# Evictions of the in-projection without the scheduling mark, and three rearrangements around the down-projection

## The chip, the cores and the metric

The kernel runs on one core of one Trainium2 chip. The metric is the device time of one execution in microseconds (us). A core has TensorE (PE in the profile, with PEld for its weight loads), VectorE (DVE), ScalarE (ACT), GpSimd (POOL) and SyncE (SP), which here issues most of the transfers. Each engine works through its own queue in order and waits on semaphores for the others. A time is told by three runs of the kernel before: 2315.92, 2316.55 and 2322.16 us, median 2316.55.

## The reference

One step of a hybrid layer, all in fp32, for 2048 prompt tokens and 8 short sample sequences of 16 tokens: 17 tiles of 128 tokens with 1024 features each. In short:

```
z = x @ w_in                    # 1024 -> mLSTM q, k, v, o-gate, gates; attention q, k, v
h = mlstm_chunkwise(...)        # 4 heads x 128, then a norm per head times the o-gate
a = swa(...)                    # 8 query heads on 2 key heads, window of two chunks, rotary, sinks
x = LN(alpha * x + concat(h, a) @ w_out)
u = causal_conv3(x @ w_up)      # 1024 -> 2 x 2816, value and gate
y = LN(alpha * x + (silu(gate) * value) @ w_down)
```

It returns y for the prompt and the samples, and the new states and key/value rows.

## The kernel before

Each fp32 operand is split in two parts that TensorE takes at full rate: `split` casts to the high part on ACT (L217) and subtracts for the low part on DVE (L218). A product is then three matmuls: high by high, high by low, low by high. The large matrix products are also cut in 2 x 2 blocks and computed with seven block products instead of eight (Winograd's form of Strassen's method). Sums of blocks are made on DVE before, and sums of results while they are evicted from PSUM. Several results share a PSUM bank by being copied from one bank to another and added onto.

The order of TensorE's instructions is written out by hand. On the other engines a scheduler orders them by what is ready and by priority. `tc.high_priority()` marks instructions so that they go ahead of others; `tc.issue_after(x)` keeps instructions behind instruction x.

Stages, in the time of the profile:

- In-projection, about 0 to 634 us (L704, `i_product`; sample tiles L714; direct tiles L730). Four token blocks b, in each five column groups g, in each seven products s of 24 matmuls with 256 columns. The products of a group run in the order 6, 7, 2, 5, (1 of the next group), 3, 4. They share three banks: A for s = 1 and 2, B for 6, 5, 3, and C for 7, 4. `i_after` evicts after each product. After s = 6 ACT copies B (the lines L763 to L771, the forms that scale, copy or apply tanh). After s = 2 it evicts A. After s = 5 it copies B and DVE adds C to it (L775, L777). After s = 3 ACT evicts B and then copies A onto B (L799), which the next group's product 6 adds to. After s = 4 DVE adds C once more. A product that writes a bank waits for those that read it. Chains of the mLSTM (L1083 to L1244: decay dt and wi, pnum, the head statistics L1149, hn, pht) and of the attention (L1303 to L1359: scores sc, softmax L1307 to L1324, ppt, pth) run between these products, with their ACT and DVE work in the same queues. POOL takes one square root of variance per head group there (L1161).
- `d_sums` runs beside the in-projection: block sums of the down-projection's weights. For each of eleven pairs k, step 0 loads two weight tiles `txy` into buffers that otherwise hold tokens (L844, L845), step 1 makes four sums of 512 columns on DVE (L850 to L853), and step 2 stores both to DRAM (`zt`, L855, L856). Eight pairs are made in blocks 2 and 3 of the in-projection, three in the output projection.
- Output projection (`o_block`), about 634 to 870 us, with the last chains (ppt L1346).
- Up-projection, about 870 to 1884 us (L1877, `f_ups`): three token blocks, 22 column pairs j, seven products. `f_evict` makes value and gate u from the banks (ACT L1898 to L1912, DVE L1906, L1908, L1914), and DVE, ACT and POOL compute the convolution and the gate (L1928 to L1960). In the last products the program already prepares the down-projection: `d_weights` loads a weight unit (L2023) and splits it into `uw`, `d_tokens` splits a token unit into `fu`.
- Down-projection, about 1847 to 2317 us (L2087, `f_downs`): for each block seven products of six units. DVE adds finished products into the rows `yacc` (L2116, L2118), and the last norm follows in pieces. The last tile is finished by `norm_last`: statistics in two halves (L1559), aggregate (L1560), a power on POOL (L1562), and then two passes over 512 columns each (L1545, L1547), stored one by one.

Of the kernel before, what the change touches and what calls it, by code (L numbers as in the profile page):

```python
# [14 lines left out]
P = 128  # L15
# [189 lines left out]
class Prog:  # L205
# [381 lines left out]
    def i_dense(self):  # L587
# [34 lines left out]
        for item in self.items:  # L622
            if after:

                after[0] -= 1
                if after[0] == 3:
                    self.logs_of(after[1] - 1)
                if after[0] < 0:
                    self.i_done = after[1]
                    after = None  # L630
            self.chains.hold = item[0] == "t" and item[1] > 0
            if item[0] == "t":
                _, b, ti, e = item
                if ("g", e, 3) not in self.wu:
                    self.advance()
                if b not in self.gates:
                    self.gates[b] = self.tp.tile([P, 5, 8], F32, name="gates", tag="gates", bufs=2)
                ps = self.bank([P, 512], "pg") if ti == 4 else self.ib[ti % 2 * 2]
                yield from self.i_direct(b, ti, e, ps)
                self.i_keys(b, ti, ps)  # L640
                if ti == 1:
                    if b + 1 < nb:
                        self.x_steps(b + 1, 1, 2)
                    else:
                        self.release(4)
# [12 lines left out]
            del self.wu[item]  # L658
            self.release(2)
            if self.trans and s != 4:  # L660
                self.i_transposes()
            with self.tc.high_priority():
                behind = self.i_after(b, g, s)
            if (b, g, s) == (0, 0, 7):
                self.t_setup()
            if (g, s) == (1, 6):
                self.rope_load(IBLOCKS[b][0], 2)
            if g == last and b + 1 < nb:
                if s == 7:
# [12 lines left out]
            if b >= nb // 2 and g < last:  # L682

                steps = (6, 2, 5) if g == last - 1 else (6, 5, 3)
                if s in steps:
                    self.d_sums(sums, steps.index(s))
                    sums += s == steps[2]
        self.sums = sums
        self.logs_of(nb - 1)
        self.chains.hold = False  # L690
# [846 lines left out]
        self.mix_out(t, 4, mix)  # L1537


    def norm_last(self, y, g, bb, dst, st):  # L1540

        nc, V = self.nc, self.nc.vector
        mv, s = self.stats(y, st)
        for c in (slice(0, 512), slice(512, 1024)):
            V.scalar_tensor_tensor(y[:, c], y[:, c], mv[:, 0:1], g[:, c], op0=ALU.subtract, op1=ALU.mult)  # L1545
        for c in (slice(0, 512), slice(512, 1024)):
            V.scalar_tensor_tensor(y[:, c], y[:, c], s[:, 0:1], bb[:, c], op0=ALU.mult, op1=ALU.add)  # L1547
            nc.sync.dma_start(dst[:, c], y[:, c])

    def stats(self, y, st=None):  # L1550
        nc = self.nc
        V = nc.vector
# [5 lines left out]
        for i in range(half, 2):  # L1558
            V.bn_stats(st[:, i], y[:, i * 512:(i + 1) * 512])  # L1559
        V.bn_aggr(mv, st)  # L1560
# [255 lines left out]
    def f_ups(self, n):  # L1816
# [11 lines left out]
        for i, (b, j, s) in enumerate(self.seq):  # L1828
# [25 lines left out]
                self.d_begin()  # L1854

            left = len(self.seq) - i
            if left in (8, 7, 5, 3, 1):
                self.d_weights()
            if left in (9, 8, 7, 6):
                self.d_tokens()  # L1860
        nc.sync.dma_start(self.a["conv_p"], self.prev.rearrange("p v j r -> p (v j) r"))
        nc.sync.dma_start(self.a["conv_s"], self.convs.rearrange("p v j b r -> p (v j) b r"))

# [15 lines left out]
    def f_evict(self, b, j, s):  # L1879
# [22 lines left out]
        elif s == 5:  # L1902
            self.ug = u = half(1)
            u4 = f2.tile([P, 384], F32, name="ub", tag="ub", bufs=1)[:, :h]
            S.copy(u4, B)
            V.tensor_add(u[:, 2 + h:2 + WP], C[:, :m], u4[:, :m])  # L1906
            if has_s:
                V.tensor_add(sam(u)[:, :, 2:], dec(C), dec(u4))  # L1908
        elif s == 3:
            S.copy(self.uv[:, 2 + h:2 + WP], B[:, :m])  # L1910
            if has_s:
# [144 lines left out]
    def f_downs(self):  # L2056
# [17 lines left out]
        nb, nu = len(FBLOCKS), len(DUNITS)  # L2074
        ys, ops = {}, {}
        last_tile = FBLOCKS[-1][0]
        st = self.wp.tile([P, 2, 6], F32, name="st", tag="st", bufs=1)

        def product(s, p, units):
            ps = banks[role[s][2 if p == np_ else p]]  # L2080
            c = slice(p * P, p * P + P)
            for u in units:
                wh, wl, fh, fl = ops[u]
                n = len(DUNITS[u])
                for k in range(n):
                    for i, (l, r) in enumerate(((fh, wh), (fh, wl), (fl, wh))):
                        mm(ps, l[:, k, c], r[:, k], start=s in (1, 4, 7) and u == 0 and k == 0 and i == 0,  # L2087
                           stop=u == nu - 1 and k == n - 1 and i == 2, skip_group_check=True)

        def after(s, p):  # L2090
# [5 lines left out]
            elif s == 2:  # L2096
                add(ta, 0, ps, True)
                if ta == last_tile:
                    V.bn_stats(st[:, 0], ys[ta][:, :512])
# [19 lines left out]

        def finish(t, b, step):  # L2120
            if b == nb - 1 and step == 3:
                self.norm_last(ys[t], *ln2, a["y"][t], st if t == last_tile else None)
                return
            y, (g, bb) = ys[t], ln2
            mv, sc = self.stats(y)
# [8 lines left out]
        for g, (b, s, u) in enumerate(self.dseq):  # L2134
# [16 lines left out]
                    product(s, p, [u])  # L2151
            elif u == 0:
                cols = cols[::-1]
                for p in cols:
                    product(s, p, [u])
            elif u == nu - 1:

                cols = cols[::-1]
                for p in cols:
                    product(s, p, range(1, nu))  # L2160
                    after(s, p)
                    for _ in pending.pop():
                        pass

            for f in pending[:2]:
                if next(f, self) is self:
# [23 lines left out]
```

## Time and profile before

| | |
|---|---|
| median of three runs | 2316.55 us (2315.92 to 2322.16) |
| the profiled execution, its own time | 2321.38 us |
| span of its trace | 2319.6 us |
| mean granted TensorE clock | 0.995 |
| busy: TensorE, weight loads | 2287.3 us, 2097.9 us |
| busy: DVE, ACT, POOL | 1818.9, 1273.3, 267.8 us |
| moved by DMA | 632.39 MB, 273 GB/s |

A row of the timeline has the start and the duration in us, the engine, the line, the operation, out <- in, and the count of instructions that the row joins; a bracket gives the idle time before the row and what released it. Consecutive instructions on one engine overlap a little, so that in a row of them each takes some 0.1 us less than the duration shown. A row of waits has the waiting instruction, what released it, the sum in us, how often, and the longest. A row of windows has the window, its length, the busy time of each engine with its count, the granted clock, the DMA share and GB/s.

### The profile page before, as it was taken

To read this page: it belongs to the slowest core of one execution; us is meant where nothing else is said; L and a number is where in the kernel's file an instruction comes from. 1 tells how busy PE (TensorE), PEld (TensorE's weight loads), DVE (VectorE), ACT (ScalarE), POOL (GpSimd) and SP (SyncE) were. 2 spreads that over 40 slices of the span, in tenths; PEclk is the share of its full clock that TensorE was granted. 3 is DMA by queue.
4 is the path that set the end of the run, shared out by engine and by line. 5 is a ranking of instruction groups with operands and counts; after the bars stand their busy time and mean duration, and the time that the engine had idled before them with its cause. 6 is when DMAs were issued, how large, how long until landed. Compare 5 with 4: busy or idle time off the path is not lost. (4 is left out here: it accounts for less than half of the span.)

```text
span 2319.6 us, 39851 instructions
## 1 busy us (share of the span) xinstructions
PE 2287.3 (99%) x14293; PEld 2097.9 (90%) x14293; DVE 1818.9 (78%) x3189; ACT 1273.3 (55%) x2409; POOL 267.8 (12%) x477
## 2 busy tenths in 40 slices
PE   8999999999999999999999999999999999999998
PEld 8999989899977778999999999999999978888876
DVE  7777687787688888998788777678766786895987
ACT  5453466776766665555556555556555544444442
POOL 0001000100011112121102000003111200100200
PEclk9999999999999999999999999999999999999999
DMA  7888999989986767788777888888998776756743
GB/s 270 289 304 294 302 311 329 313 300 327 334 279 225 234 210 271 286 327 310 279 293 270 307 306 307 314 269 283 313 297 265 227 286 205 258 176 218 258 153 109
DMA packets 300166, 632.39 MB, mean 273 GB/s; under 512 B 47868, under 2 KB 141120, under 8 KB 299968
## 3 DMA queue, kind: packets, MB, share of 16 engines
q1 hardware_dynamic: 295296, 616.14, 77.5%
q0 software_dynamic: 3520, 10.56, 1.4%
q10 hardware_dynamic: 1152, 3.15, 0.4%
q8 instruction: 113, 1.85, 0.3%
q14 instruction: 85, 0.70, 0.1%
HBM read 458.11 MB, written 171.64 MB: 271 GB/s over the span
## 5 line engine op out<-in xcount | busy, mean ns | idle before, releaser
L1877 PE MATMUL dps<-hh,uw 128*128 128x384 f32 (+1 forms) x1848 | 478.1, 328 | 2.6 <-DVE u L1908 2.0
L1877 PE MATMUL fup<-hh,uw 128*128 128x384 f32 (+1 forms) x1848 | 478.1, 328 | 0.3 <-ACT ua L1898 0.2
L1877 PEld LDWEIGHTS dps<-hh,uw 128*128 128x128 f32 x1848 | 329.9, 188 | 3.1 <-DVE u L1908 2.3
L1877 PEld LDWEIGHTS fup<-hh,uw 128*128 128x128 f32 x1848 | 330.0, 188 | 0.8 <-ACT ua L1898 0.5
L1934 DVE SCALAR_TENSOR_TENSOR cc<-u,cw,cc 128x768 f32<-128x768 f32 (+1 forms) x264 | 258.2, 979 | 60.9 <-ACT cc L1932 51.8
L1877 PE MATMUL fup<-hl,uw 128*128 128x384 f32 (+1 forms) x924 | 302.5, 327 | 1.8 <-DVE hl L218 1.8
L1877 PE MATMUL dps<-hl,uw 128*128 128x384 f32 (+1 forms) x924 | 302.3, 327 | 0.0
L704 PE MATMUL dps<-w,oh 128*128 128x256 f32 x1344 | 254.9, 284 | 1.2 <-DMA w<-zws 0.7
L217 ACT CAST uw<-wraw 128x1024 fp32r<-128x1024 f32 x126 | 123.1, 979 | 222.8 <-PE dps L2087 120.1
L218 DVE TENSOR_TENSOR w<-wraw,w 128x1024 fp32r<-128x1024 f32 (+2 forms) x167 | 189.3, 1141 | 50.4 <-ACT w L217 45.7
L704 PEld LDWEIGHTS dps<-w,oh 128*128 128x128 f32 x1344 | 210.6, 188 | 12.7 <-issue 8.1
L217 ACT CAST w<-wraw 128x1024 fp32r<-128x1024 f32 (+2 forms) x167 | 163.2, 984 | 102.9 <-PE dps L704 37.3
L218 DVE TENSOR_TENSOR uw<-wraw,uw 128x1024 fp32r<-128x1024 f32 x126 | 142.5, 1132 | 64.3 <-ACT uw L217 64.3
L704 PE MATMUL dps<-w,ol 128*128 128x256 f32 x672 | 187.9, 280 | 0.0
L704 PE MATMUL dps<-oh,w 128*128 128x256 f32 x896 | 172.5, 287 | 6.2 <-ACT mr L1152 3.4
L1877 PEld LDWEIGHTS fup<-hl,uw 128*128 128x128 f32 x924 | 173.5, 188 | 2.5 <-DVE hl L218 2.4
L2087 PE MATMUL fup<-uw,fu 128*128 128x512 f32 x726 | 174.0, 396 | 0.6 <-DVE uw L218 0.6
L1877 PEld LDWEIGHTS dps<-hl,uw 128*128 128x128 f32 x924 | 173.5, 188 | 0.0
L2087 PEld LDWEIGHTS fup<-uw,fu 128*128 128x128 f32 x726 | 136.3, 188 | 34.0 <-DVE uw L218 1.1
L2087 PE MATMUL dps<-uw,fu 128*128 128x512 f32 x660 | 165.3, 396 | 1.1 <-DVE uw L218 1.1
L1932 ACT ACTIVATE cc<-u,cw 128x768 f32<-128x768 f32 (+1 forms) x132 | 132.2, 1001 | 52.6 <-DVE u L1914 26.7
L704 PEld LDWEIGHTS dps<-oh,w 128*128 128x128 f32 x896 | 143.5, 192 | 12.7 <-issue 4.1
(322 smaller groups left out, 4588.6 us busy)
## 6 DMA issues: line engine op xcount, KB each, us to landing
uw<-zw SPq DMA_DIRECT2D x176, 512.0 KB, 5.2
zw<-uw SPq DMA_DIRECT2D x88, 512.0 KB, 3.6
w<-zws SPq DMA_DIRECT2D x72, 512.0 KB, 6.4
wv<-wup SPq DMA_DIRECT2D x66, 512.0 KB, 4.8
wraw<-wi SPq DMA_DIRECT2D x65, 512.0 KB, 5.3
wraw<-zt SPq DMA_DIRECT2D x60, 512.0 KB, 4.3
wraw<-wdn SPq DMA_DIRECT2D x45, 512.0 KB, 4.2
wraw<-wo SPq DMA_DIRECT2D x40, 512.0 KB, 4.7
```

The source lines that it names most:

```text
L217: nc.scalar.copy(hi, src)
L218: nc.vector.tensor_sub(lo, src, hi.bitcast(F32))
L704: mm(o, l, r, start=s in (1, 7) and c == k == i == 0, stop=k == 3 and i == 2, skip_group_check=True)
L1877: mm(ps, l[:, k], r[:, k], start=s in (1, 7) and k == 0 and i == 0, stop=k == 3 and i == 2, skip_group_check=True)
L1932: S.activation(c[:, v], u[:, 2:2 + n], AF.Identity, bias=w[3], scale=w[2])
L1934: V.scalar_tensor_tensor(c[:, v], u[:, i:i + n], w[i], c[:, v], op0=ALU.mult, op1=ALU.add)
L2087: mm(ps, l[:, k, c], r[:, k], start=s in (1, 4, 7) and u == 0 and k == 0 and i == 0, stop=u == nu - 1 and k == n - 1 and i == 2, skip_grou ...
```

## The change

Four edits:

1. `i_after` is called without `high_priority`, so that the scheduler treats evictions as it treats other work.
2. The steps of `d_sums` stand behind other products: load after s = 7, sums after s = 3, store after s = 4. The first of the eight pairs moves from block 2 to the fourth group of block 1; the next three stay in block 2, the last four in block 3.
3. In the last products of the up-projection the calls of `d_tokens` and `d_weights` are placed otherwise, and two calls of `d_weights` and one of `d_tokens` are kept behind the last sums onto u (`u4_add`).
4. The last product of the last tile (s = 3, p = 0) is done in two halves of 256 columns. The second half's partial sum is copied by ACT to another bank at the product's first unit. The 33 matmuls of 512 columns become 66 of 256. The first half is added and its statistics are taken beside the second half's matmuls; after the last matmul stand an add and statistics of 256 columns and the aggregate over four groups.

```diff
-            with self.tc.high_priority():
-                behind = self.i_after(b, g, s)
+            behind = self.i_after(b, g, s)
...
-            if b >= nb // 2 and g < last:
-                steps = (6, 2, 5) if g == last - 1 else (6, 5, 3)
-                if s in steps:
-                    self.d_sums(sums, steps.index(s))
-                    sums += s == steps[2]
+            if s in (7, 3, 4) and (b == nb - 1 and g < last or b == nb - 2 and g < last - 1 or b == 1 and g == last - 2):
+                self.d_sums(sums, (7, 3, 4).index(s))
+                sums += s == 4
...
-            if left in (8, 7, 5, 3, 1):
+            if left in (9, 8, 7):
+                self.d_tokens()
+            if left in (8, 7):
                 self.d_weights()
-            if left in (9, 8, 7, 6):
-                self.d_tokens()
+            if left in (4, 2):
+                with self.tc.issue_after(self.u4_add):
+                    self.d_weights()
+                    if left == 4:
+                        self.d_tokens()
+            if left == 1:
+                self.d_weights()
...
-            V.tensor_add(u[:, 2 + h:2 + WP], C[:, :m], u4[:, :m])
+            z = V.tensor_add(u[:, 2 + h:2 + WP], C[:, :m], u4[:, :m])
             if has_s:
-                V.tensor_add(sam(u)[:, :, 2:], dec(C), dec(u4))
+                z = V.tensor_add(sam(u)[:, :, 2:], dec(C), dec(u4))
+            self.u4_add = z.ins
...
-        def product(s, p, units):
-            ps = banks[role[s][2 if p == np_ else p]]
+        def product(s, p, units, cs=slice(0, 512), ps=None):
+            ps = banks[role[s][2 if p == np_ else p]][:, cs] if ps is None else ps
...
-                        mm(ps, l[:, k, c], r[:, k], start=s in (1, 4, 7) and u == 0 and k == 0 and i == 0,
+                        mm(ps, l[:, k, c], r[:, k, cs], start=s in (1, 4, 7) and u == 0 and k == 0 and i == 0,
...
+                halves = [(slice(i * 256, i * 256 + 256), banks[(role[s][0], 0)[i]][:, :256]) for i in range(2)]
+                S.copy(halves[1][1], banks[role[s][0]][:, 256:])
                 for p in cols:
-                    product(s, p, [u])
+                    for cs, ps in halves if p == 0 else [(slice(0, 512), None)]:
+                        product(s, p, [u], cs, ps)
...
-                for p in cols:
+                for p in cols[:-1]:
                     product(s, p, range(1, nu))
                     after(s, p)
                     for _ in pending.pop():
                         pass
+                for i, (cs, ps) in enumerate(halves):
+                    product(s, 0, range(1, nu), cs, ps)
+                    y = ys[last_tile][:, 512 + i * 256:768 + i * 256]
+                    V.scalar_tensor_tensor(y, y, ALPHA, ps, op0=ALU.mult, op1=ALU.add)
+                    V.bn_stats(st[:, 2 + i], y)
+                self.norm_last(ys[last_tile], *ln2, a["y"][last_tile], st)
```

The statistics tile `st` of the last tile accordingly has four groups instead of two, and its first half is taken in two pieces of 256 columns.

More of the change, by code (lines that the diff above doesn't have):

```diff
@@ L1537, in swa_sample, with norm_last @@
         self.mix_out(t, 4, mix)
-    def norm_last(self, y, g, bb, dst, st):
+    def norm_last(self, y, g, bb, dst, st=None):
         nc, V = self.nc, self.nc.vector
@@ L1557, in stats @@
         s = self.wp.tile([P, 2], F32, name="lsc", tag="lsc", bufs=2)
-        for i in range(half, 2):
-            V.bn_stats(st[:, i], y[:, i * 512:(i + 1) * 512])
+        if st.shape[1] == 2:
+            for i in range(half, 2):
+                V.bn_stats(st[:, i], y[:, i * 512:(i + 1) * 512])
         V.bn_aggr(mv, st)
@@ L2076, in f_downs @@
         last_tile = FBLOCKS[-1][0]
-        st = self.wp.tile([P, 2, 6], F32, name="st", tag="st", bufs=1)
-        def product(s, p, units):
-            ps = banks[role[s][2 if p == np_ else p]]
+        st = self.wp.tile([P, 4, 6], F32, name="st", tag="st", bufs=1)
+        def product(s, p, units, cs=slice(0, 512), ps=None):
+            ps = banks[role[s][2 if p == np_ else p]][:, cs] if ps is None else ps
             c = slice(p * P, p * P + P)
@@ L2098, in after @@
                 if ta == last_tile:
-                    V.bn_stats(st[:, 0], ys[ta][:, :512])
+                    for i in range(2):
+                        V.bn_stats(st[:, i], ys[ta][:, i * 256:i * 256 + 256])
             elif s in (4, 6):
```

2 lines of the change are left out of this document (1 added, 1 removed).

## The prediction

> **What bounds the kernel now.** I read the page's busy times first, then the chain of waits of TensorE (PE), then windows with the granted clock, then the timelines at each place where an engine's order changes.
>
> The page, and TensorE's waits by the line that waited and what released it (total us, times, longest):
>
> ```profile
> PE 2287.3 (99%) x14293; PEld 2097.9 (90%) x14293; DVE 1818.9 (78%) x3189; ACT 1273.3 (55%) x2409; POOL 267.8 (12%) x477
> ...
> L704 PEld LDWEIGHTS dps<-w,oh 128*128 128x128 f32 x1344 | 210.6, 188 | 12.7 <-issue 8.1
> ...
> PE dps L704 <- ACT mr L1152: 3.4, 1, 3.4
> PE dps L1877 <- DVE u L1908: 2.0, 1, 2.0
> ...
> PE ppt L1346 <- ACT sc L1324: 1.5, 1, 1.5
> ...
> PE ppt L1521 <- POOL scs L1515: 0.8, 1, 0.8
> ...
> PE fup L2087 <- DVE uw L218: 0.6, 1, 0.6
> ...
> PE pht L1178 <- ACT hn L1168: 0.5, 1, 0.5
> ```
>
> PE is busy 2287.3 of 2319.6 us, so 32 us of idle time is all that reordering can win, besides time lost to a low clock. The windows (length, PE, PEld, DVE, ACT, POOL, granted clock, DMA share, GB/s) show that loss:
>
> ```profile
> 328.60:332.40 3.80, 0.36 (x4) 0.15 (x3) 3.65 (x15) 1.70 (x5) 0.00 (x0) 0.80 0.73 243
> 332.40:337.60 5.20, 5.20 (x24) 5.20 (x25) 5.20 (x15) 2.49 (x6) 0.00 (x0) 0.50 1.08 306
> ...
> 692.50:696.00 3.50, 3.50 (x13) 2.93 (x12) 3.01 (x9) 2.67 (x8) 1.59 (x2) 0.53 1.00 369
> ...
> 1840.00:1850.00 10.00, 8.00 (x46) 7.12 (x45) 9.91 (x15) 5.18 (x8) 6.11 (x8) 1.00 0.52 172
> ```
>
> After the 3.44 us wait the clock is 0.50 for 5.2 us, half of which is lost; behind the 1.5 us wait, which ends just before 692.5, it is 0.53 for 3.5 us (1.7 lost). The window of 1840 holds the 2.0 us wait (PE 8.00 of 10.00) at clock 1.00, so a wait of that length need not cost more than itself. The Trainium skill ("TensorE: Matmul & The Clock Gate", HAM oscillation) allows idle gaps up to about 3.4 us. The first wait agrees; the one of 1.5 us does not. By that rule alone the stalls of 1 to 2 us that I find below never halve the clock; by the rows they may (second rival).
>
> **The change, part by part.** *Evictions without the mark, and sums moved.* Both act through the queues of ACT and DVE, so they are walked together. Decisive rows, up to the late head (ACT, DVE, PE, POOL timelines):
>
> ```profile
> 316.63 0.59 ACT L771 ACTIVATE zev<-dps 128x512 f32<-128x512 f32 x1
> ...
> 320.48 0.39 ACT L1318 ACTIVATE sc<-sc,amx 128x128 f32<-128x128 f32 x1
> ...
> 326.87 1.27 ACT L1324 ACTIVATE sc<-sc,asm 128x128 f32<-128x128 f32 x4
> ...
> 320.91 0.67 DVE L1131 TENSOR_TENSOR dt<-pscore,dt 128x512 f32<-128x512 f32 x1
> 321.51 1.20 DVE L218 TENSOR_TENSOR w<-wraw,w 128x1024 fp32r<-128x1024 f32 x1
> ...
> 327.27 0.69 DVE L850 TENSOR_TENSOR txy<-txy 128x512 f32<-128x512 f32 x1 [3.32 <-DMA txy<-wdn]
> ...
> 320.55 0.39 PE L704 MATMUL dps<-oh,w 128*128 128x256 f32 x2
> ...
> 320.89 0.39 PE L704 MATMUL dps<-oh,w 128*128 128x256 f32 x2
> ...
> 321.69 1.13 PE L1213 MATMUL pnum<-v,dt 128*128 128x129 f32 x8 [0.18 <-issue]
> ...
> 328.66 0.28 PE L704 MATMUL dps<-oh,w 128*128 128x256 f32 x1
> 332.38 0.58 PE L704 MATMUL dps<-oh,w 128*128 128x256 f32 x1 [3.44 <-ACT mr L1152]
> ...
> 341.22 0.75 PE L1178 MATMUL pht<-ident,hn 128*128 128x128 f32 x4
> ...
> 337.78 1.47 POOL L1161 TENSOR_TENSOR ms<-mq,mhalf 128x4 f32<-128x4 f32 x1 [13.64 <-DVE mq L1160]
> ```
>
> The 3.44 us stall begins on DVE: it waits 3.32 us at L850 for a weight tile (issued too late for its place), so L1149's statistics and ACT's mr (L1152) are late, and the eviction L771 stands behind them. The change puts that pair's sums elsewhere, so the DVE wait leaves. But L771 of 316.63 now stands behind five attention activations (L1316, four L1318) of which the last ends at 320.9; with its own 0.59 it ends near 321.5, while the product that overwrites its bank began at 320.66 (the second matmul of the row of 320.55): new stall 0.8. On DVE the split (1.20) now precedes dt (L1131): it ends about 322.7 and the pnum of 321.69 begins near 322.8 (these 1.1 us include the 0.8). The next two products end at 330.05 instead of 328.94. The second L771 (it ended just before the 332.38) now follows eight L1324 softmax divisions, one cast and both mr on ACT. From 327.0, where ACT's earlier work ends in the new order, that is 8 x 0.3 (1.27 for four) + 1.0 for the cast (as 1.20 on DVE, a little less on ACT) + 0.2 + 0.6: about 331.2, and I allow 331.0 to 331.5. So a stall of 1.0 to 1.5 replaces 3.44, and I take the clock to stay at 1.00, nearest to the 2.0 us wait that left it there. What is late next is pht (341.22). It needs hn, which needs the statistics (on DVE until about 335.5 behind two splits), POOL's 1.47, a small DVE product, and four ACT operations at 0.3: pht's last input comes at about 338.5 and pht stands at 338.7. Gain 2.5; bounds 0.2 if the clock still halves, and 3.8 if hn is in time and only PE's own work counts.
>
> The first weight pair moves a block earlier, to about 167 to 178 us: its two loads take SP places of two token loads, four DVE sums like L850 (0.69 each, 2.7 us) stand among small gate operations, two stores follow, and the two displaced token loads wait behind these stores and a dozen weight loads on SP; their tokens belong to the next block, more than 100 us on. Queued behind the sums on DVE are two weight splits. PE's weights are split some four products ahead, and a product is 24 matmuls at 0.34/3 us (320.55 to 320.89: three), about 2.8 us, so the sums are hidden and I cost them 0; if that cover is gone, 2.7. The following pairs occupy the places of their predecessors (0). Around 394 to 411 one pair (2.7 us of DVE and its load wait) leaves, and the hn wait there goes: gain 0.5, between 0 and 0.5. At 253 the sampled-attention chain passes an eviction: the POOL wait goes, gain 0.8, bounds 0 and 0.8. Losses follow at two places where an eviction falls behind other work:
>
> ```profile
> 369.48 0.59 ACT L799 COPY dps<-dps 128x512 f32<-128x512 f32 x1
> 369.99 0.69 ACT L1168 ACTIVATE hn<-hn,ms 128x128 f32<-128x128 f32 x2
> 370.58 1.04 ACT L217 CAST w<-wraw 128x1024 fp32r<-128x1024 f32 x1
> ...
> 371.42 0.28 PE L704 MATMUL dps<-w,oh 128*128 128x256 f32 x1
> ...
> 573.56 0.68 DVE L777 TENSOR_TENSOR zev<-dps,zev 128x512 f32<-128x512 f32 x1
> ...
> 574.22 0.68 DVE L1131 TENSOR_TENSOR dt<-pscore,dt 128x512 f32<-128x512 f32 x1
> ...
> 575.49 0.68 DVE L1206 TENSOR_TENSOR qk<-qk,wi 128x512 f32<-128x512 f32 x1
> ...
> 574.63 0.40 PE L704 MATMUL dps<-w,oh 128*128 128x256 f32 x2
> ```
>
> L799 now comes after the two hn and the cast, so it ends near 371.7, 0.3 after the product of 371.42 wants its bank (0 to 0.4). L777 comes after L1131 and L1206 (0.6 each in a row) and one tiny operation: it ends near 575.5 instead of 574.2, and the product that begins with the second matmul of 574.63 stalls 0.8 (0.2 to 0.9). Elsewhere in blocks 0 to 3 the moved evictions keep slack on the walked queues (0, at worst 0.5 at 58 us).
>
> *The last up-projection.* Sums u (L1908) now precede the splits of later down-projection weights:
>
> ```profile
> 1844.37 0.29 DVE L1908 TENSOR_TENSOR u<-dps,ub 128x128 f32<-128x128 f32 x1
> ...
> 1894.15 2.01 PE L2087 MATMUL dps<-uw,fu 128*128 128x512 f32 x8
> ...
> 1891.92 1.22 DVE L218 TENSOR_TENSOR uw<-wraw,uw 128x1024 fp32r<-128x1024 f32 x1
> 1893.05 1.98 DVE L2116 SCALAR_TENSOR_TENSOR yacc<-yacc,fup 128x512 f32<-128x512 f32 x3
> ```
>
> Two weight splits of 1.22 (1.13 in a row) step back, so L1908 ends near 1842.4 instead of 1844.66: the 2.0 stall goes (at worst 0.2 of it stays). Queued behind the waiting L1908 are those two splits, of the third and fourth down-projection unit; at 18 matmuls a unit PE asks for the third some 8 us after the down-projection begins, so they have room. On SP two weight loads fall behind the stores of the convolution state, which wait for POOL; their splits stand after those of four earlier units (0). The split that fup L2087 waited 0.6 for moves up thirteen places on DVE: that stall goes. Late next is the split of 1891.92: it now follows the three L2116, the last of which needs the product that ends at 1894.15 in old time. From that moment 0.88 us of L2116 and 1.1 of split remain, of which one matmul covers 0.23: new stall 1.8. Net 2.64 - 1.8 = gain 0.8; bounds 2.6, and a loss of 0.9 if this stall is followed by low clock at the price of the one at 692 (1.7, half of 3.5).
>
> *The last result in halves.* The chain after the last matmul, with L1908's 0.29 at 128 columns above:
>
> ```profile
> 2312.20 0.69 DVE L2116 SCALAR_TENSOR_TENSOR yacc<-yacc,fht 128x512 f32<-128x512 f32 x1 [1.27 <-PE fht L2087]
> 2312.93 0.69 DVE L1559 BATCH_NORM_STATS2 st<-yacc 128x6 f32<-128x512 f32 x1
> 2313.65 0.21 DVE L1560 BATCH_NORM_AGGREGATE lmv<-st 128x2 f32<-128x12 f32 x1
> ```
>
> Between 0.29 at 128 and 0.69 at 512 columns, 256 should take about 0.42 in each of the first two, and the aggregate over four groups a little more than 0.21 (I take 0.25): gain 2 x 0.27 - 0.04 = 0.5, bounds 0.3 and 0.7. The first half's two operations run beside the second half's 33 matmuls. Fifteen casts still follow the added ACT copy in ACT's order, so its bank is ready long before PE adds to it (0; if not, its own length, under 0.59). The 66 narrow matmuls cost 0: L704's, equally narrow and each with its own weights, run three in 0.34 us, though one weight load is shown as 188 ns: the loads are hidden. Against this, the same page of the Trainium skill (The mechanism) lets a load overlap running matmuls only when the row group differs, and gives 128/1.2, about 107 ns, for one: by it the 33 extra loads would add 3.5 us, an estimate. The L704 rows contradict it.
>
> **The sum.** -2.5 (316 to 341) -0.8 (253) -0.5 (409) +0.3 (371) +0.8 (574) -0.8 (1842 to 1894) -0.5 (end) = -4.0 us. Against the profiled execution's own 2321.4 that is 2317.4; this execution stands 4.8 above the median 2316.55, so the forecast is 2312.5, 0.17% less. Of this kernel 0.3%, about 7 us, is what a measurement can tell from no change.
>
> **Rivals.** *More gain.* hn is in time (another 1.3), the stall at 1892 does not come because DVE reaches the split earlier (1.8), and the low clock after 689, whose wait stays, falls away with the shifted moment (1.7): -4.0 - 4.8 = -8.8, 2307.8. For it: two low stretches exist and hang on the moment of a wait. Against: POOL's 1.47 stands in the hn chain. 0.31.
>
> *Clock gate.* The stalls of 1 to 1.8 at 331 and 1892 halve the clock as the one at 689 did: +2.3 and +1.7, so 0.0: 2316.6. For: 692's 0.53; against: 1840's 1.00. 0.14.
>
> *Slower: evictions late everywhere.* With the mark gone each bank handover queues behind a cast or activations as L799 does at 371 (0.3 to 0.4). Blocks 1 to 3 have 15 column groups with three bank handovers each. It decides (over +7) from 29 of the 45 at 0.38; at 33 of them 12.5 - 4.0 = +8.5, 2325. Against: L799 itself had 1.35 us of slack (370.07 to 371.42) and loses it only because 1.7 us of work passes it; most moved evictions are passed by one or two instructions. 0.13.
>
> *Weight loads not hidden.* 33 x 188 ns = 6.2: +2.2, 2318.8. 0.03. That the change does nothing is excluded: the order on ACT and DVE does change.
>
> **Numbers.** My forecast has 0.39. Faster: the first rival and a little of the forecast's better bounds, 0.33. Slower 0.13 plus 0.01. The rest, 0.53, within 7 us. The range reaches from 2305.5 (first rival with the better bounds at 1894 and the end) to 2320.5 (weight loads, plus 1.7 of low clock). The likeliest's own range is 2309.5 to 2316.
>
> **What would show it.** Right: no wait near 1842; at 331 a wait under 1.6 at clock 1.00; waits on zev near 320 and 574; one on uw near 1892; the end of the last matmul to the aggregate at 0.9 rather than 1.45. Wrong: a low clock at 331, new waits on zev in many groups, or weights late near 180 us.

## The result, and the profile after

| | before | after |
|---|---|---|
| median of 22 runs each | 2317.99 us (2313.71 to 2323.13) | 2322.13 us (2318.25 to 2326.77) |
| ratio | | 1.0020, 95% interval 1.0014 to 1.0027 |
| profiled execution, its own time | 2321.38 us | 2318.83 us |
| span, mean granted clock | 2319.6 us, 0.995 | 2317.0 us, 0.999 |

The changed kernel is 4.1 us slower, 0.2%. That is within the 0.3% that the prediction called no change, but it lies above the range (2305.5 to 2320.5) and on the other side of the forecast of 2312.5. The two profiled executions point the other way because that of before lies high among its own runs and that of after almost at the bottom of its own; so stretches are compared below, and not ends.

The waits of TensorE in the changed kernel (waiting line, releaser: total us, times, longest):

```profile
PE dps L2094 <- DVE uw L218: 2.8, 2, 1.7
PE dps L701 <- ACT zev L768: 2.0, 3, 1.0
...
PE dps L701 <- DMA w<-zws: 1.8, 3, 1.2
PE dps L701 <- ACT dps L796: 1.7, 2, 0.9
PE ppt L1343 <- ACT sc L1321: 1.4, 1, 1.4
...
PE fup L2094 <- ACT fht L2102: 0.8, 1, 0.8
...
PE dps L701 <- DVE zev L774: 0.7, 1, 0.7
```

The long waits of before (3.4 on mr, 2.0 on u) are gone; one of 1.7 and several of about 1 us came. TensorE's timeline puts places to them:

```profile
59.41 0.39 PE L701 MATMUL dps<-oh,w 128*128 128x256 f32 x1 [0.78 <-ACT dps L796]
...
257.74 0.51 PE L701 MATMUL dps<-w,oh 128*128 128x256 f32 x2 [1.21 <-DMA w<-zws]
...
321.26 0.39 PE L701 MATMUL dps<-oh,w 128*128 128x256 f32 x1 [0.28 <-ACT zev L768]
...
322.64 1.13 PE L1210 MATMUL pnum<-v,dt 128*128 128x129 f32 x8 [0.41 <-issue]
...
330.72 0.39 PE L701 MATMUL dps<-oh,w 128*128 128x256 f32 x1 [1.03 <-ACT zev L768]
...
369.57 0.38 PE L701 MATMUL dps<-w,oh 128*128 128x256 f32 x1 [0.94 <-ACT dps L796]
...
573.54 0.39 PE L701 MATMUL dps<-w,oh 128*128 128x256 f32 x1 [0.75 <-DVE zev L774]
...
1868.40 23.27 PE L2094 MATMUL fup<-uw,fu 128*128 128x512 f32 x99 [0.77 <-ACT fht L2102]
...
1893.59 2.83 PE L2094 MATMUL dps<-uw,fu 128*128 128x512 f32 x11 [1.68 <-DVE uw L218]
```

Most of that is near the walk of the prediction (the differences come at the end). What the walk did not look for stands in windows where TensorE waits for nothing and the clock is 1.00 (window, length, PE, PEld, DVE, ACT, POOL, clock, DMA share, GB/s). Before:

```profile
180.00:230.00 50.00, 50.00 (x437) 46.16 (x436) 37.52 (x77) 18.29 (x32) 10.17 (x7) 1.00 0.83 291
1900.00:2200.00 300.00, 300.00 (x1287) 241.36 (x1286) 245.52 (x305) 133.91 (x165) 28.49 (x24) 1.00 0.67 221
```

After:

```profile
180.00:230.00 50.00, 50.00 (x426) 46.16 (x425) 37.32 (x77) 17.46 (x30) 10.17 (x7) 1.00 0.92 328
1900.00:2200.00 300.00, 300.00 (x1292) 242.42 (x1291) 244.80 (x305) 132.19 (x163) 26.48 (x24) 1.00 0.67 222
...
328.60:332.00 3.40, 2.37 (x20) 2.16 (x19) 3.40 (x16) 3.25 (x9) 0.00 (x0) 1.00 1.09 355
332.00:338.00 6.00, 5.99 (x50) 5.48 (x48) 5.06 (x11) 3.66 (x8) 1.47 (x1) 1.00 1.04 362
```

From 180 to 230 us the same 50.00 us of full work at the same granted clock hold 426 matmuls instead of 437. From 1900 to 2200 us it is the other way, 1292 instead of 1287. Such a count can miss a record; so for each run I took the mean time from the start of one matmul to the start of the next, wherever there is no gap and no low clock. I call it the pace:

| ns per matmul | before | after | difference x count |
|---|---|---|---|
| in-projection, 256 columns | 116.67 | 118.38 | +1.71 x 3360 (4 blocks, 5 groups, 7 products of 24) = +5.7 us |
| up-projection, 384 columns | 174.52 | 174.96 | +0.44 x 3696 = +1.6 us |
| down-projection, 512 columns | 233.35 | 232.44 | -0.91 x 1980 = -1.8 us |

The sum is +5.5 us. TensorE's work as a whole has grown by more. Its busy time is 2287.3 before, and after it is

```profile
PE 2288.4 (99%) x14326; PEld 2101.1 (91%) x14326; DVE 1820.6 (79%) x3192; ACT 1273.5 (55%) x2410; POOL 257.8 (11%) x477
```

A part of either is low clock, and before has more of it. Besides the stretches behind the waits at 331 and 689, which after lacks, both executions have some in their first 50 us. The windows of the first 100 us, before and then after, have a clock of 0.95 and 0.98:

```profile
0.00:100.00 100.00, 92.67 (x702) 89.38 (x703) 72.24 (x98) 48.18 (x71) 0.31 (x5) 0.95 0.78 274
...
0.00:100.00 100.00, 91.55 (x704) 88.05 (x705) 72.92 (x99) 48.20 (x71) 0.31 (x5) 0.98 0.78 275
```

The traces show a clock of 0.50 in all of these stretches. Half of the time in which TensorE is busy in them is 9.3 us before and 1.4 after. Without that half its work is 2278.0 and 2287.0 us, 9.0 more; the three rows of the table are 5.5 of this, the output projection some 1.0 (283.9 and 284.9), and the rest has no row. Idle time falls by 3.7 (from 2319.6 - 2287.3 = 32.3 to 2317.0 - 2288.4 = 28.6). So waits and clock give 3.7 + 7.9 = 11.6 in this pair of executions, the longer work takes 9.0 back, and the spans differ by 2.6. The low clock differs from one execution to the next, the work hardly does, and in the medians the loss is the larger. The experiments ask which edit brings the slower pace, and why.

### The profile page after: what moved, and what is told of

Same layout as the page of the kernel before. It is cut to its first block, busy times and chain, and to the rows that moved or that the text cites. A ratio compares the mean times of both kernels' runs of the same rounds, so it can differ in the third digit from the quotient of the medians.

```text
span 2317.0 us, 39914 instructions
## 1 busy us (share of the span) xinstructions
PE 2288.4 (99%) x14326; PEld 2101.1 (91%) x14326; DVE 1820.6 (79%) x3192; ACT 1273.5 (55%) x2410; POOL 257.8 (11%) x477
## 5 line engine op out<-in xcount | busy, mean ns | idle before, releaser
L217 ACT CAST uw<-wraw 128x1024 fp32r<-128x1024 f32 x126 | 123.1, 978 | 219.4 <-PE dps L2094 118.3
L2094 PE MATMUL fup<-uw,fu 128*128 128x512 f32 (+1 forms) x759 | 177.6, 390 | 0.8 <-ACT fht L2102 0.8
L2094 PEld LDWEIGHTS dps<-uw,fu 128*128 128x128 f32 x660 | 123.9, 188 | 32.7 <-DVE uw L218 3.6
```

Source lines behind the costliest of these rows:

```text
L217: nc.scalar.copy(hi, src)
L2094: mm(ps, l[:, k, c], r[:, k, cs], start=s in (1, 4, 7) and u == 0 and k == 0 and i == 0, stop=u == nu - 1 and k == n - 1 and i == 2, skip_ ...
```

## The experiments

Each batch has its own runs of the kernel before on the same chip. The ratios are estimates over all runs, with a 95% interval (the plain ratio of the two medians differs by up to 0.0006); 0.1% is 2.3 us. The pace is given as above.

**One edit at a time.** The four edits of the diff, each alone on the kernel before. First the mark:

```diff
-            with self.tc.high_priority():
-                behind = self.i_after(b, g, s)
+            behind = self.i_after(b, g, s)
```

> The kernel before with edit 1 alone (evictions unmarked). Theory A, the evictions make the changed kernel slower: the profile of the changed kernel has new TensorE waits of 0.8 (59 us), 1.2 (257), 0.3 + 0.4 (322), 1.0 (331), 0.9 (370) and 0.75 (574), 5.3 us in all; with edit 1 alone they should be there while the late weight tile still costs its wait near 330, so +3 to +7 us. Theory B, the moved weight sums are the cause: edit 1 alone is within 1.5 us of before.

The weight sums:

```diff
-            if b >= nb // 2 and g < last:
-                steps = (6, 2, 5) if g == last - 1 else (6, 5, 3)
...
+            if s in (7, 3, 4) and (b == nb - 1 and g < last or b == nb - 2 and g < last - 1 or b == 1 and g == last - 2):
+                self.d_sums(sums, (7, 3, 4).index(s))
```

> The kernel before with edit 2 alone (weight sums behind other products, the first pair a block earlier), evictions still marked. Theory A: the 3.4 us wait near 330 and the low clock behind it leave and nothing comes in their place, -2 to -5 us. Theory B, the sums in block 1 and the loads that stand behind them delay evictions, splits or weight loads: +3 to +6 us, with waits between 170 and 260 us.

The last up-projection:

```diff
-            if left in (8, 7, 5, 3, 1):
+            if left in (9, 8, 7):
+                self.d_tokens()
+            if left in (8, 7):
                 self.d_weights()
...
+            if left in (4, 2):
+                with self.tc.issue_after(self.u4_add):
+                    self.d_weights()
```

> The kernel before with edit 3 alone (weight and token splits at the end of the up-projection rearranged). From the profile of the changed kernel: the waits of 2.0 and 0.64 go, waits of 0.8 (1868) and 1.7 (1894) come, so -0.2 us and no difference that can be measured under theories A and B. Rival: the new waits are longer in most executions or halve the clock, +1.5 to +4 us.

The last result in halves:

```diff
-        st = self.wp.tile([P, 2, 6], F32, name="st", tag="st", bufs=1)
+        st = self.wp.tile([P, 4, 6], F32, name="st", tag="st", bufs=1)
...
+                for i, (cs, ps) in enumerate(halves):
+                    product(s, 0, range(1, nu), cs, ps)
```

> The kernel before with edit 4 alone (last result in halves of 256 columns). The chain after the last matmul shortens by about 0.5 us: -0.5 us under theories A and B. Rival: the 66 narrow matmuls cost more than 33 wide ones, which would show as a longer last product: +1 to +3 us.

| edit alone | median, before 2316.34 | ratio | pace of the in-projection |
|---|---|---|---|
| mark | 2316.03 | 0.9996 (0.9987 to 1.0005) | 116.54 |
| sums | 2317.79 | 1.0006 (0.9996 to 1.0016) | 116.56 |
| up-projection | 2315.25 | 0.9993 (0.9984 to 1.0002) | 116.56 |
| halves | 2321.39 | 1.0021 (1.0010 to 1.0032) | 118.38 |

The whole loss belongs to the edit that touches only the last 10 us, and it is taken in stages far from it: its paces in the three stages, 118.38, 174.95 and 232.42, are those of the changed kernel. So neither of the two theories with which these runs began, late evictions or the moved sums, is the cause. The mark alone cures the wait at 331: TensorE's waits with the mark taken away have

```profile
PE dps L703 <- ACT zev L770: 2.4, 3, 1.1
```

three waits of at most 1.1 and none on mr. On DVE the first weight sum of that pair, with its place in the program as before, now comes after the statistics L1148, and without a wait for its tile (DVE timeline):

```profile
325.43 0.47 DVE L1148 BATCH_NORM_STATS2 bst<-pnum 128x6 f32<-128x128 f32 x2
...
330.80 0.68 DVE L849 TENSOR_TENSOR txy<-txy 128x512 f32<-128x512 f32 x1
```

With the sums moved alone, DVE still waits for the weight tile (its timeline), and TensorE waits as before (its waits):

```profile
327.03 0.69 DVE L848 TENSOR_TENSOR txy<-txy 128x512 f32<-128x512 f32 x1 [2.99 <-DMA txy<-wdn]
```

```profile
PE dps L702 <- ACT mr L1150: 3.1, 1, 3.1
```

The third edit alone takes away the waits of 2.0 and 0.6 and brings the new one of 1.68 (TensorE's timeline):

```profile
1862.04 23.31 PE L2096 MATMUL fup<-uw,fu 128*128 128x512 f32 x99 [0.43 <-ACT fht L2104]
...
1887.26 2.83 PE L2096 MATMUL dps<-uw,fu 128*128 128x512 f32 x11 [1.68 <-DVE uw L218]
```

**What of the halves slows the in-projection.** The only thing of this edit that exists before the end is `st`, which grows from 12 to 24 numbers in each partition, 48 to 96 bytes. In the built program tiles take whole steps of 32 bytes, `st` is the last tile of its pool, and all pools that lie behind it on its side of SBUF move up by 32 bytes. (The other tiles of its own pool stay, among them the buffers of the weights `w`, which begin 64 bytes past a multiple of 128; so do the tiles of the other side.) The token tiles all began at multiples of 128 bytes; the first `oh`, that began at byte 75776 (592 x 128), begins at 75808. So `st` alone was made larger, on the kernel before, with nothing else changed. By 32 bytes:

```diff
-        st = self.wp.tile([P, 2, 6], F32, name="st", tag="st", bufs=1)
+        st = self.wp.tile([P, 4, 6], F32, name="st", tag="st", bufs=1)[:, :2]
```

> The kernel before, with only the statistics tile st enlarged from 12 to 24 numbers per partition, of which it uses the first 12 as before. All later tiles of the left side of SBUF then lie 32 bytes further, off a 64-byte boundary. Theory C (the addresses cost): the gap from one 256-column matmul of the in-projection to the next rises from about 116.8 to 118.3 ns as in the changed kernel, and the time by +4 to +7 us. Rival D (the split product itself costs): no change, 0 within 1 us.

By 64 bytes (the tile of 128 bytes, the same 12 numbers used):

```diff
+        st = self.wp.tile([P, 32], F32, name="st", tag="st", bufs=1)[:, :12].rearrange("p (a b) -> p a b", b=6)
```

> The kernel before, with st enlarged to 32 numbers per partition, so that later tiles lie 64 bytes further, on a 64-byte boundary again. Theory C by alignment: 0 within 1.5 us, cadence near 116.8 ns. If any move of addresses costs, +4 to +7 us. Rival D: 0.

The same 64 bytes in the changed kernel, and with the halves alone (`[P, 32]`, 24 numbers used):

> The changed kernel with st padded to 32 numbers per partition, later tiles on 64-byte boundaries. Theory C: the four edits without the shift, -1 to -4 us against before (the sum of edits 1 to 3 measured alone is about 0, edit 4 gives 0.5). Rival D: still +4 us.

> The kernel before with edit 4 alone and st padded to 32 numbers per partition. Theory C: -0.5 us, same within the interval. Rival D: +5 us as edit 4 measured with the shift.

And on the kernel before, with `[P, 48]`, `[P, 80]` and `[P, 40]`, by 128, 256 and 96 bytes:

> The kernel before with st enlarged so that later tiles of the left side lie 128 bytes further. In the kernel before the token tiles begin at multiples of 2048 bytes. Theory C1 (a start on 128 bytes is enough): 0 within 1.5 us and 116.8 ns between narrow matmuls. Theory C2 (a coarser start, or this very place, counts): +4 to +7 us and 118 ns or more, as with 32 and 64 bytes.

> The same with 256 bytes. If 128 bytes cost and 256 do not, the start has to be on 256: 0 within 1.5 us and 116.8 ns. If both cost, only a coarser start or the very place of before is good: +4 to +7 us.

> The kernel before with st enlarged so that later tiles of the left side lie 96 bytes further. Moves of 0, 128 and 256 bytes left the in-projection at 116.5 to 116.7 ns, moves of 32 and 64 gave 118.4 to 118.8. If the place within 128 bytes counts: 118 ns or more and +4 to +7 us. If only 32 and 64 are bad: 116.5 ns and 0.

| tiles moved by | on | ratio | in-projection | up | down |
|---|---|---|---|---|---|
| 32 bytes | before | 1.0025 (1.0014 to 1.0036) | 118.53 | 174.95 | 232.43 |
| 64 | before | 1.0029 (1.0019 to 1.0038) | 118.79 | 174.96 | 233.20 |
| 64 | all edits | 1.0018 (1.0008 to 1.0028) | 118.76 | 174.96 | 233.24 |
| 64 | halves | 1.0028 (1.0018 to 1.0038) | 118.78 | 174.97 | 233.20 |
| 96 | before | 1.0022 (1.0012 to 1.0032) | 118.27 | 174.56 | 233.32 |
| 128 | before | 1.0014 (1.0006 to 1.0023) | 116.51 | 174.61 | 233.67 |
| 256 | before | 1.0002 (0.9991 to 1.0014) | 116.59 | 174.53 | 233.37 |

The windows of the kernel before with a larger `st`, and no other change, show it, by 32 bytes:

```profile
180.00:230.00 50.00, 50.00 (x426) 46.16 (x425) 36.90 (x76) 17.43 (x30) 10.17 (x7) 1.00 0.80 283
1900.00:2200.00 300.00, 300.00 (x1293) 242.36 (x1292) 245.86 (x305) 134.44 (x165) 28.49 (x24) 1.00 0.66 220
```

and by 256:

```profile
180.00:230.00 50.00, 50.00 (x437) 46.13 (x436) 38.02 (x78) 18.28 (x29) 10.18 (x7) 1.00 0.85 301
```

My next thought after the first move, that multiples of 64 bytes are good, fell with the second row: 64 is as bad as 32. Moves of 32, 64 and 96 are bad for the in-projection and 128 and 256 are not, which fits a period of 128 bytes. The move by 128 has the good pace and yet 1.0014: its profile has low clock for 6.8 us at 332 and 3.4 us at 693, but the kernel before has the same two. Its paces in the other two stages come to +0.9 us (0.09 x 3696 and 0.32 x 1980); what remains above that is not explained.

**Which tiles.** The 32 bytes were put at other places by an unused tile, on the kernel before: ahead of the in-projection's token tiles (the eviction tiles and the output projection's own tiles move along, those of the up- and down-projection keep their places), ahead of the eviction tiles behind them, or ahead of the tiles of the down-projection that TensorE does not read.

```diff
             self.xp, xcm = enter("xsb")
+            self.xp.tile([P, 8], F32, name="pad", tag="pad", bufs=1)
```

> The kernel before with 32 bytes put in ahead of the in-projection's own pools: token tiles (and the eviction tiles behind them) move by 32 bytes, all tiles of the up- and down-projection stay. If the place of the token tiles against the weight tiles sets the cadence: 118.4 ns in the in-projection, 174.5 and 233.35 ns in the later stages as before, and +4 to +7 us. Rival (the later stages carry the loss): 0 within 1.5 us.

```diff
             self.mp, mcm = enter("isb")
+            self.mp.tile([P, 8], F32, name="pad", tag="pad", bufs=1)
```

> The kernel before with 32 bytes put in behind the token tiles, so that only the tiles of the in-projection's evictions and rotary tables move; token tiles, weights and all later stages stay. If the place of what TensorE reads counts: 0 within 1.5 us, 116.8 ns. If the place of what ACT, DVE and the transfers touch counts: a rise toward 118 ns and +3 to +6 us.

```diff
             self.f2, f2cm = enter("dsb")
+            self.f2.tile([P, 8], F32, name="pad", tag="pad", bufs=1)
```

> The kernel before with 32 bytes put in ahead of the down-projection's own pool, which holds only tiles that TensorE does not read. If only what TensorE reads counts: 233.35 ns in the down-projection as before and 0 within 1.5 us. Rival: 232.4 ns, as the shift of everything gave, and -1.9 us.

| ahead of | ratio | in-projection | up | down |
|---|---|---|---|---|
| token tiles | 1.0022 (1.0012 to 1.0033) | 118.39 | 174.54 | 233.36 |
| eviction tiles | 0.9996 (0.9987 to 1.0005) | 116.41 | 174.52 | 233.40 |
| `yacc` and its like | 1.0001 (0.9992 to 1.0011) | 116.58 | 174.52 | 233.34 |

The pool of the token tiles carries the loss: moved with what lies behind it up to the output projection it gives the whole size, the eviction tiles alone give nothing, and the two other stages keep their pace. Besides TensorE's operands `oh` and `ol` this pool holds tiles that TensorE does not read (raw tokens, `txy`); they were not moved by themselves. Their windows, moved:

```profile
180.00:230.00 50.00, 50.00 (x425) 46.16 (x425) 34.79 (x70) 16.93 (x31) 10.18 (x7) 1.00 0.73 263
1900.00:2200.00 300.00, 300.00 (x1287) 241.35 (x1286) 245.94 (x307) 132.10 (x162) 24.52 (x24) 1.00 0.66 222
```

and the eviction tiles moved instead:

```profile
180.00:230.00 50.00, 50.00 (x436) 46.16 (x435) 35.51 (x72) 18.16 (x32) 10.18 (x7) 1.00 0.81 288
```

The balance of the result's section, TensorE's busy time without half of what is under low clock, sorts all 20 profiles in the same way. It is 2275.1 to 2280.2 us in the twelve in which the token tiles begin at a multiple of 128 bytes, and 2283.6 to 2287.0 in the eight in which they do not.

The traces also tell in which use the tiles are slow. In the first two column groups of a block the weights are loaded into TensorE and the tokens' 256 columns stream past them (rows `oh,w` and `ol,w`, 1344 matmuls); in the other three the tokens are loaded and the weights stream (rows `w,oh` and `w,ol`, 2016 matmuls). The paces of the two kinds:

| ns per matmul, token tiles moved by | tokens stream | tokens are loaded |
|---|---|---|
| 0, 128, 256 bytes | 115.1 to 115.7 | 117.0 to 117.2 |
| 32 | 119.2 to 119.6 | 117.9 |
| 64 | 119.0 | 118.7 to 118.8 |
| 96 | 117.9 | 118.5 |

Both uses are slower, and at 32 bytes most of the loss comes where the tokens stream: 3.6 x 1344 = 4.8 us in the changed kernel, against 0.7 x 2016 = 1.4.

**What the edits are worth by themselves.** The changed kernel with its 24 numbers kept in the buffer of another tile (`cw`, free by then), so that all other tiles stay where before has them:

```diff
-        st = self.wp.tile([P, 4, 6], F32, name="st", tag="st", bufs=1)
+        self.wp.tile([P, 2, 6], F32, name="st0", tag="st", bufs=1)
+        st = self.fp.tile([P, NUP, 4], F32, name="st", tag="cw", bufs=1).rearrange("p a b -> p (a b)")[:, :24].rearrange("p (a b) -> p a b", b=6)
```

> The changed kernel with its statistics tile st put into a buffer that the up-projection has finished with, and the old room of st left empty: every other tile lies as in the kernel before. If the move of addresses is all that makes the changed kernel slower, this gives the four edits' own worth: my forecast was -4.0; by edits 1 to 3 measured alone (-0.9, +1.4, -1.6) and 0.5 for edit 4 it is -1.6. A rival (the edits together cost): still +3 us or more.

The same without the moved sums, and the mark and the up-projection alone:

> Edits 1, 3 and 4 without edit 2, with all other tiles at their places of before. Edit 1 alone already brought the wait near 330 from 3.4 to 1.1 us, edit 2 alone left it at 3.1. If edit 2 is not needed: -2 to -4 us against before. If the edits 1, 3 and 4 have no worth of their own: 0 within 2 us.

> Edits 1 and 3 alone; no tile moves. From the runs of each alone (-0.9 and -1.6): -2.5 us. If the low clock comes as often as before: 0 within 1.5 us.

| at the old places | ratio | in us | forecast by the same terms |
|---|---|---|---|
| all four | 1.0007 (0.9998 to 1.0016) | +1.6 (-0.5 to +3.7) | -4.0 |
| without the sums | 0.9993 (0.9982 to 1.0004) | -1.6 (-4.2 to +0.9) | -3.5 |
| mark and up-projection | 0.9996 (0.9986 to 1.0006) | -0.9 (-3.2 to +1.4) | -3.0 |

All four have the pace of before again (window 180 to 230):

```profile
180.00:230.00 50.00, 50.00 (x437) 46.16 (x436) 36.84 (x76) 17.73 (x30) 10.18 (x7) 1.00 0.91 325
```

So at the old places the loss is not there; but neither is the gain. Without the sums the forecast lies inside the interval, and so does zero; with them it lies outside. The profile with the sums has waits that the one without lacks, such as

```profile
536.18 0.39 PE L701 MATMUL dps<-w,oh 128*128 128x256 f32 x1 [1.06 <-ACT dps L796]
```

but others of its waits lie where the sums cannot reach, and it is one execution: that the sums cost some 3 us (from -1.6 to +1.6) is suggested and not shown; the intervals overlap, and alone on the kernel before they gave 1.0006, between -0.9 and +3.7 us.

**A version from what was learnt.** The kernel without the moved sums at the old places, with the weight slots of the down-projection (and only these of TensorE's operands) moved by 32 bytes, and the up-projection's own tiles behind them by 128 in all:

```diff
             self.wx, wxcm = enter("wx2sb")
+            self.wx.tile([P, 8], F32, name="pad", tag="pad", bufs=1)
...
             self.f2, f2cm = enter("f2sb")
+            self.f2.tile([P, 24], F32, name="pad2", tag="pad2", bufs=1)
```

> Edits 1, 3 and 4 with the tiles at their places of before, except that the two weight slots of the up- and down-projection above the shared pool move by 32 bytes and the up-projection's own tiles by 128. The shift of everything had brought the down-projection from 233.35 to 232.4 ns a matmul, and the pool of tiles that TensorE does not read had no part in it. If those two weight slots are what did it: 232.4 ns in the down-projection (2013 matmuls, -1.9 us), 174.5 in the up-projection, and -2.6 to -5 us against before in all. If not: 233.35 and -1 us, or slower if the up-projection suffers.

It ran in 2313.74 us (2310.54 to 2317.67) against 2316.48, ratio 0.9989 (0.9980 to 0.9999): faster than before, by an interval that just leaves out 1 (one of 18 comparisons, so it can be chance; the 2.7 us between the medians lie at the near end of what was expected, 2.6 to 5). Against the same edits without the move (0.9993) the times do not tell it apart; the paces do. Its windows have the good pace of each stage (116.44, 174.41 and 232.43 ns):

```profile
180.00:230.00 50.00, 50.00 (x436) 46.16 (x435) 36.31 (x76) 18.16 (x32) 10.19 (x7) 1.00 0.81 292
1900.00:2200.00 300.00, 300.00 (x1293) 242.43 (x1292) 243.83 (x303) 133.09 (x164) 24.50 (x24) 1.00 0.67 223
```

## Why the prediction was wrong

**The step that failed** is "The last result in halves". It costed the edit by the rows of the last 10 us: two operations shortened, a copy in the shadow of casts, matmuls with hidden weight loads. The list of what the edit adds stopped at instructions. It also adds 48 bytes to a tile, which moves the in-projection's token tiles off a multiple of 128 bytes; the term is +5.5 us by the pace, and 1.0021 to 1.0029 (4.9 to 6.7 us) in the runs that move these tiles by 32 or 64 bytes without the other edits. No row of before could price it, but the diff showed the tile, and that every address behind it moves could have been seen. None of the rivals was this: the slower one, late evictions in 29 of 45 handovers, did not happen. Alone, this edit was forecast at -0.5 us and measured +4.9 (2.3 to 7.4).

That is not the whole miss. The other three edits were forecast at -3.5 together; alone they measured -0.9, +1.4 and -1.6, -1.1 in sum, each to within about 2, and all four at the old places +1.6 instead of -4.0. So the forecast gain is not in the medians either, and the intervals leave open how the 8.1 us between -4.0 and +4.1 divide.

**The end itself was right.** The last add, statistics and aggregate after (DVE timeline):

```profile
2308.63 0.41 DVE L2179 SCALAR_TENSOR_TENSOR yacc<-yacc,fht 128x256 f32<-128x256 f32 x1
...
2310.02 0.42 DVE L2179 SCALAR_TENSOR_TENSOR yacc<-yacc,fup 128x256 f32<-128x256 f32 x1 [0.52 <-PE fup L2094]
2310.48 0.43 DVE L2180 BATCH_NORM_STATS2 st<-yacc 128x6 f32<-128x256 f32 x1
2310.94 0.26 DVE L1558 BATCH_NORM_AGGREGATE lmv<-st 128x2 f32<-128x24 f32 x1
```

From the add to the aggregate it is 0.92 instead of 1.45. The narrow matmuls were right as well:

```profile
2306.64 3.35 PE L2094 MATMUL fup<-uw,fu 128*128 128x256 f32 x27
```

27 of them, each with its own weights, take 3.35 us, the last one's latency included. At 118 ns each that is 3.2. So the rival of weight loads that are not hidden fell. With it falls, for this row, the sentence of the Trainium skill ("TensorE: Matmul & The Clock Gate", The mechanism) that a load overlaps only where the row group differs: by the page's 107 ns for a load the 27 would take about 6 us, an estimate. The same section also lets a load go ahead if it fills the background weight buffer, and that the row does not contradict.

**316 to 341 us.** The wait went from 3.44 to 1.03 (forecast 1.0 to 1.5) and the clock behind it stayed at 1.00; near 321 there are 0.28 and 0.41 (forecast 1.1 together). TensorE's order is the same in both kernels there: from its first matmul after 316 us to the pht of 341 it took 25.2 us before and 21.3 after (21.6 with the mark alone). The gain of 3.9 is not the forecast 2.5 but its upper bound (3.8): the pht waits for nothing (at most 0.2 with the mark alone), so hn was in time, a part of the first rival. The reason was wrong in one point: "The change puts that pair's sums elsewhere, so the DVE wait leaves". The DVE wait does leave, but not by that edit. With the sums moved alone DVE still waits 2.99. With the mark alone taken away the scheduler puts the first of these sums behind the statistics (330.80 instead of 327.27), DVE does not wait for its tile, and TensorE's wait is 1.1.

**The other terms.** 409 went, as forecast, and the POOL wait of 253 too, but beside it stands 1.21 at 257 for a weight tile still on its way, a price that "the POOL wait goes" left out; it appears in this profile alone. 574 is 0.75 for 0.8. 371 is 0.94 for 0.3, outside its bounds (0 to 0.4). ACT's queue was walked rightly there: from the first of the hn to the end of the copy L796 (L799 before) it is 3.2 us in the trace and 3.3 in the walk. But TensorE asks for the bank 2.1 us after that hn began, where before it was 3.0 (371.42 - 368.40), and the walk had left that distance as it was. 59 is 0.78 for "at worst 0.5". In the last up-projection 1894 is 1.68 for 1.8, and the wait at 1842 is gone; the 0.77 at 1868, on ACT's copy, was missed. Of the six other profiles with that edit three have it, with 0.4, 0.4 and 1.5: a term that the sum lacked.

**The clock gate rival** (stalls of 1 to 1.8 halve the clock) did not come at 331 or 1894. Over all profiles, those of before and after among them, the wait at 331 of 2.0 to 3.5 us (evictions marked) is followed by a low clock in 10 of 13, and that of 1.0 to 1.3 us (unmarked) in none of 7. The rule of the Trainium skill (the same page, HAM oscillation), that gaps up to about 3.4 us are safe, does not hold here. The wait of 1.5 at 689 is followed by it in 4 of 20 profiles, and that of 2.0 at 1842 in 3 of 13; that of 1.7 at 1894 in none of 7. So a wait of such a length has a chance of it and no certainty; one low stretch, at 237 us in the run with the eviction tiles moved, even follows two waits of only 0.87 and 0.70. The prediction's reading of 1840 ("a wait of that length need not cost more than itself") is true of one execution. The low clock at 331 lasted 6.8 us in two of the ten, that of before among them, and 3.4 in eight. Half of TensorE's busy time in it is 1.4 us as a mean over the 13. The forecast took 2.6 off a median, the price of one long stretch.

## What to carry to other kernels

An edit that changes the size of any tile is also an edit of every tile allocated after it: list those addresses, and look whether TensorE's operands move within 128 bytes, before costing the edit by its instructions. Compare the pace of matmuls in stretches without waits first; it shows in one window a loss that no row of waits shows. One execution's low clock after a wait is a chance and not a price.

## What the runs showed of the hardware

The pace of a matmul at full clock depends on where its operands start. In the in-projection, with the token tiles `oh` and `ol` at a multiple of 128 bytes it is 116.4 to 116.7 ns, moved by 32, 64 or 96 bytes 118.3 to 118.8. It does so whether the tokens stream through TensorE (115.1 to 115.7 against 117.9 to 119.6) or are loaded into it (117.0 to 117.2 against 117.9 to 118.8). The up-projection's 384 columns have 174.4 to 174.6 after moves of 0, 96, 128 and 256 bytes, and 175.0 after 32 and 64. The down-projection's 512 columns have 232.4 with the two weight slots moved by 32 bytes, and 233.2 to 233.7 in all other places that were tried. The granted clock is 1.00 in all of these. A multiple of 128 bytes is not the rule for every operand: the down-projection became faster with two of its weight slots moved off one, and the in-projection's weights `w` begin 64 bytes past one in all of these runs. Since they never moved, the runs do not tell whether the tokens' own place counts or their place against the weights. Why it matters was not tried: whether it is how TensorE reads an operand, a meeting with another engine's or a transfer's accesses, or something else stays open, as does whether other offsets are better still than those of before.
